# The last slot of a mixture-of-experts block: when the slot in front is added to its first chunk, and in which order the last two chunks are normalised

## Chip, cores and metric

The kernel runs on one core of a Trainium2 chip. The metric is the device time of one execution in microseconds (us), as the median of several executions. The engines are named as the profile names them: PE (TensorE, the matrix products), PEld (its weight loads), DVE (VectorE), ACT (ScalarE), POOL (GpSimd) and SP (SyncE, which here only issues transfers).

## What is computed

512 tokens of width 1024 pass through a mixer block, a layer norm, a mixture of 32 experts (two experts for each token) together with a gated per-layer term, and a last layer norm. Only the end of it matters here:

```python
h = _layernorm(DEEPNORM_ALPHA * h + mix, ln1_g[i], ln1_b[i])
moe = _hier_moe(h, ...)      # for each expert: act = silu(h @ gate) * (h @ up) * weight;  out += act @ down
ple = (p[i] @ w_ple[i]) * jax.nn.sigmoid(h @ w_pg[i] + b_pg[i])
h = _layernorm(DEEPNORM_ALPHA * h + moe + ple, ln2_g[i], ln2_b[i])
```

## The kernel before

The tokens stand in `tok` as four chunks of 128 rows by 1024 columns, float32. The experts are worked off in 12 slots of 128 gathered token rows; a slot holds the rows of a few experts side by side. For each slot `gate_up` multiplies the gathered rows with the gate and up weights in two halves (`kh` 0 and 1, each over four of the eight pieces of the width), `act` makes silu(gate) * up * weight, `atr` transposes it, and `down` multiplies it with the down weights into two banks of 512 columns each. After each bank ScalarE copies it out (`yh`, line 1105) and VectorE forms what the copy rounded away (`yl`, line 1107); the slot's result is the sum of the two.

`scatter(s, chunks)` adds the result of slot `s` back to the chunks: for each chunk and each half of 512 columns one product of a 0/1 matrix with `yh` (line 1142), one with `yl` (line 1144) and one VectorE addition to `tok` (line 1145). It is issued for the slot in front while the next slot is at work.

The last slot (`last_slot`, slot 11, with `p` = 10 the slot in front) is arranged by hand. The token rows that the last slot itself works on are put together separately, in the two banks `zr`, from their earlier share (`take`) and the slot's own products (`take_own`); for all other rows the four chunks of `tok` are complete as soon as slot `p` is added. The chunks are normalised and stored while the last slot's products go on. Each chunk needs: two statistics passes and an aggregation on VectorE (`ln_dve`), a square root on ScalarE (`ln_sqrt`), a reciprocal (`ln_rs`), and then the two passes that apply mean, scale, gain and offset, in one of two ways:

- `ln_pool`: `ln_nm` on VectorE (a 128x1 value), then for each 512 columns a pass on ScalarE (line 1392) and a multiplication on GpSimd (line 1393), and a GpSimd addition (line 1395). Chunk 0, chunk 1 and the first 512 columns of chunk 3 go this way. The second half of chunk 1 is called from inside `act`, behind the sigmoid.
- `affine_a` and `affine_b`: two VectorE passes, both with two inputs in the on-chip memory (lines 1400 and 1405). Chunk 2 and the last 512 columns of chunk 3 go this way.

At the end `put` writes chunk 3 by an indirect transfer issued from GpSimd; then the sums in `zr` are normalised on VectorE (lines 1465 to 1472) into `row`, and a second `put` writes these rows. The first `put` waits for both halves of chunk 3.

Each engine works through its instructions in the order in which the kernel's code issues them (`tc.manual_schedule()`), and waits for other engines by semaphores; so the order of the calls in `last_slot` is the order on every engine. The accumulation banks of the scatter products are three in turn, shared with those of `down`; a bank is free when VectorE has read it.

Of the kernel before, what the change touches and what calls it, by code (L numbers as in the profile page):

```python
# [140 lines left out]
def block_kernel(ctx: ExitStack, tc: tile.TileContext, I, out):  # L141
# [14 lines left out]
    def pst(tag, nm="", shape=(P, 512), dt=F32):  # L156
        _pi[0] += 1
        banks[tag].append(banks[tag].pop(0))
        return ps.tile(list(shape), dt, tag=f"b{banks[tag][-1]}", name=f"{tag}{_pi[0]}_{nm}")

    def sm(nm, *shape, dt=F32, tag=None, bufs=1):
        return small.tile([P, *shape], dt, tag=tag or nm, bufs=bufs, name=nm)
# [30 lines left out]
    def ln_part(key, src, h, n=2):  # L193
        if h == 0:
            stt_[key] = sm(f"st{key}", n, 6, tag=f"st{n}", bufs=4)
        V.bn_stats(stt_[key][:, h, :], src[:, h * (D // n):(h + 1) * (D // n)])
# [7 lines left out]
    def ln_rs(key):  # L204
        V.reciprocal(rst[key], rst[key])

    def ln_nm(key):
        nmt[key] = sm(f"nm{key}", 1, tag="nm", bufs=4)
        V.tensor_scalar(nmt[key], mvt[key][:, 0:1], rst[key], -1.0, OP.mult, OP.mult)
# [467 lines left out]
    def done(*keys):  # L677
        for k in keys:
            tag = W.pop(k)[1]
            if tag is None:  # L680
                continue
            if tag == "bc" and len(pieces) < 26:
                bc2.append(tmp("bc", 1, [P, 2, D], "bc2"))
            elif k[0] == "x" and k[2] == YK and not ytags:
                ytags.append(tag)
            else:
                free.append(tag)
        pump()
# [351 lines left out]
    def gate_up(s, lanes, kh, mid=None):  # L1040
        if kh == 0:
            gps[s] = pst("g" if s < NS else "u", f"gu{s}")
        g = gps[s]
        for k in range(4 * kh, 4 * kh + 4):
            if mid and k % 4 == 2:
                mid()
            for q, m, r in lanes:
                PE.matmul(g[q:q + m, :], xTs[s][:, k, q:q + m],  # L1048
                          W["x", r, kh][0][:, (k % 4) * 512:(k % 4 + 1) * 512],
                          start=(k == 0), stop=(k == KD - 1), tile_position=(0, q))  # L1050
        clk["pe"] += 3.7
        done(*[("x", r, kh) for r in dict.fromkeys(r for _, _, r in lanes)])

    def act(s, wsl, tkf, i, oh=None, sa=None):
        g = gps[s]
        sa = tmp("ct", 2, [P, 2, F], f"sa{s}") if sa is None else sa
        A.activation(sa[:, 0, :], g[:, 0:F], AF.Sigmoid)  # L1057
        if s == NS - 1:
            ln_pool(1, 512, D)
        V.tensor_mul(sa[:, 0, :], g[:, 0:F], sa[:, 0, :])  # L1060
        V.scalar_tensor_tensor(sa[:, 1, :], g[:, F:2 * F], wsl[:, i:i + 1], sa[:, 0, :], OP.mult, OP.mult)
        acts[s] = sa
        if s == NS - 1:
            return
        if s in DS:
            return
        ohs[s] = tmp("cv", 2, [P, T], f"oh{s}", F32R) if oh is None else oh
        V.tensor_scalar(ohs[s], C["iota"], tkf[:, i:i + 1], None, OP.is_equal)

    def atr(s, dst=None):  # L1070
        pt = pst("t", f"at{s}")
        for c in range(2):
            PE.transpose(pt[:, c * P:(c + 1) * P], acts[s][:, 1, c * P:(c + 1) * P], idn)  # L1073
        aTs[s] = tmp("full", 2, [P, 2, P], f"aT{s}") if dst is None else dst
        A.copy(aTs[s], pt[:, 0:2 * P].rearrange("p (c t) -> p c t", t=P))
# [58 lines left out]
    def scatter(s, cs=range(NC), mid=None, hs=(0, 1)):  # L1134
        yh, yl = ys[s]
        for c in cs:
            for h in hs:
                if mid and h:
                    mid()
                w = slice(h * 512, (h + 1) * 512)  # L1140
                o = pst("u", f"sc{s}{c}{h}")
                PE.matmul(o, ohs[s][:, c * P:(c + 1) * P], yh[:, w], start=True, stop=yl is None)  # L1142
                if yl is not None:
                    PE.matmul(o, ohs[s][:, c * P:(c + 1) * P], yl[:, w], start=False, stop=True)  # L1144
                V.tensor_add(tok[:, c, w], tok[:, c, w], o)  # L1145
            clk["pe"] += 1.15
# [213 lines left out]
    def take(key, rows, start=False):  # L1360
        for h in range(2):
            for i in range(2):
                PE.matmul(zr[h], sel[key], rows[i][:, h * 512:(h + 1) * 512], start=start and i == 0, stop=False)  # L1363

    def take_own(h):
        PE.matmul(zr[h], sel["own"], ys[NS - 1][:, h, :], start=False, stop=True)


    def ln_dve(c):

        key = f"2{c}"
        for h in range(2):
            ln_part(key, tok[:, c, :], h)
        mvt[key] = sm(f"mv{key}", 2, tag="mv", bufs=4)
        V.bn_aggr(mvt[key], stt_[key])
        nmt[key] = None

    def ln_sqrt(c):
        key = f"2{c}"
        rst[key] = sm(f"rs{key}", 1, tag="rs", bufs=4)  # L1380
        A.activation(rst[key], mvt[key][:, 1:2], AF.Sqrt, bias=eps_t)

    def ln_pool(c, lo, hi):

        key = f"2{c}"
        if nmt[key] is None:
            ln_nm(key)
        nm = nmt[key]
        for a in range(lo, hi, 512):
            b = min(a + 512, hi)  # L1390
            t = tok[:, c, a:b]
            A.activation(t, t, AF.Identity, bias=nm, scale=rst[key])
            G.tensor_mul(t, t, bc2[0][:, 0, a:b])
        t = tok[:, c, lo:hi]
        G.tensor_add(t, t, bc2[0][:, 1, lo:hi])

    def affine_a(c, lo=0, hi=D):

        t = tok[:, c, lo:hi]
        V.scalar_tensor_tensor(t, t, mvt[f"2{c}"][:, 0:1], bc2[0][:, 0, lo:hi], OP.subtract, OP.mult)  # L1400

    def affine_b(c, lo=0, hi=D):

        t = tok[:, c, lo:hi]
        V.scalar_tensor_tensor(t, t, rst[f"2{c}"], bc2[0][:, 1, lo:hi], OP.mult, OP.add)  # L1405
# [3 lines left out]
    def store(c, lo=0, hi=D):  # L1409
        stores.append(SP.dma_start(out[c * P:(c + 1) * P, lo:hi], tok[:, c, lo:hi]))  # L1410

    def put(to, rows):
        return G.indirect_dma_start(out=out, out_offset=bass.IndirectOffsetOnAxis(ap=to[:, 0:1], axis=0),
                                    in_=rows, in_offset=None, bounds_check=T - 1, oob_is_err=False)

    def last_slot(lanes):
        s = NS - 1
        p = s - 1
        A.activation(warm, eps_t, AF.Sqrt)

        def first():
            scatter(p, (0,))
            ln_dve(0)
            ln_sqrt(0)
            scatter(p, (1,))
            ln_rs("20")
            ln_pool(0, 0, D)
            store(0)

        gate_up(s, lanes, 0, first)  # L1430
        ln_dve(1)
        ln_sqrt(1)
        scatter(p, (2,))
        gate_up(s, lanes, 1)
        A.activation(warm, eps_t, AF.Sigmoid)
        ln_rs("21")
        ln_pool(1, 0, 512)
        ln_dve(2)
        act(s, wsl, tkf, s)
        scatter(p, (3,))  # L1440
        take(p, ys[p])
        atr(s)
        ln_sqrt(2)
        ln_dve(3)
        ln_sqrt(3)
        ln_rs("22")
        affine_a(2)
        affine_b(2)
        store(2)
        store(1)  # L1450
        ln_rs("23")
        ln_nm("23")
        affine_a(3, LNP)
        affine_b(3, LNP)
        down(s, lanes)
        ln_pool(3, 0, LNP)
        s3 = put(sel["to3"], tok[:, NC - 1, :])
        for d in stores:
            tc.declare_no_dep(s3.ins, d.ins, reason="rows of other chunks")
        for h in range(2):  # L1460
            take_own(h)
        key = "2r"
        stt_[key] = sm("st2r", 2, 6, tag="st2", bufs=4)
        for h in range(2):
            V.bn_stats(stt_[key][:, h, :], zr[h])
        ln_var(key)
        row = tmp("x0", 1, [P, D], "row")
        for h in range(2):
            t = row[:, h * 512:(h + 1) * 512]
            V.scalar_tensor_tensor(t, zr[h], mvt[key][:, 0:1], bc2[0][:, 0, h * 512:(h + 1) * 512], OP.subtract, OP.mult)  # L1470
        ln_rs(key)
        V.scalar_tensor_tensor(row, row, rst[key], bc2[0][:, 1, :], OP.mult, OP.add)
        tc.declare_no_dep(put(sel["to"], row).ins, s3.ins, reason="disjoint rows")
# [19 lines left out]
    for s in range(NS):  # L1493
        lanes = SLOTS[s]
# [88 lines left out]
LNP = 512  # L1583
# [30 lines left out]
```

## Time and profile before

| | us |
|---|---|
| median of 3 runs | 466.48 |
| lowest and highest run | 465.04, 468.22 |
| the profiled execution, its own time | 465.6 |
| its span, first to last instruction | 463.6 |
| PE busy | 428.5 (92% of the span) |
| DVE busy | 239.2 (52%) |
| POOL busy | 149.7 (32%) |
| ACT busy | 136.0 (29%) |
| mean granted TensorE clock | 0.982 of full speed |

The span starts with the first instruction and ends with the last; the time of the execution has 2.0 us more around it. Busy shares are averages over the whole program. Times of single instructions below are microseconds from the span's start.

### The profile page before, as it was taken

Reading aid. Unit: us, or ns where it says so; the run is one execution under the profiler, and the core shown is the slowest. Engines: PE = TensorE matmul, PEld = TensorE weight load, DVE = VectorE, ACT = ScalarE, POOL = GpSimd, SP = SyncE. Lnnn points to the kernel's source line nnn. Section 1 sums busy time; section 2 is a strip of 40 time slices with the busy share of each in tenths; the row PEclk is TensorE's granted clock in tenths of the full one; section 3 lists DMA queues with packets and bytes.
Section 4 is the critical chain, followed back from the end, with each engine's and each line's share of the span. In section 5 each row is a group of like instructions: output and inputs, shape, how many; then the busy total and the mean of one; then the engine's idle time right before and its main releaser. Section 6 shows DMA issues by size and latency. Waiting matters only on the chain.

```text
span 463.6 us, 6886 instructions
## 1 busy us (share of the span) xinstructions
PE 428.5 (92%) x2583; PEld 287.6 (62%) x2583; DVE 239.2 (52%) x463; ACT 136.0 (29%) x240; POOL 149.7 (32%) x129
## 2 busy tenths in 40 slices
PE   7899977999999998899999997999999999899980
PEld 6798865788899997653556362745465544445330
DVE  4938599879764578513315010110122469735695
ACT  4453502432410377411111120111420142231360
POOL 2556499334600760130001010110040133242094
PEclk9999998999999999999999998999999999999995
DMA  8822203422769669669999999999999999999213
GB/s 270 351 92 91 92 0 98 176 90 92 260 264 386 222 258 345 246 240 418 423 419 419 420 417 426 419 419 420 422 414 418 418 420 413 417 419 396 99 57 142
DMA packets 25117, 136.85 MB, mean 295 GB/s; under 512 B 4167, under 2 KB 4427, under 8 KB 11768
## 3 DMA queue, kind: packets, MB, share of 16 engines
q1 hardware_dynamic: 20456, 124.64, 67.0%
q0 software_dynamic: 3760, 8.05, 4.6%
q10 hardware_dynamic: 864, 3.67, 2.0%
q8 instruction: 22, 0.36, 0.3%
q14 instruction: 15, 0.12, 0.1%
HBM read 134.61 MB, written 6.82 MB: 305 GB/s over the span
## 4 chain that ended last, share of the span: by engine, by line
PE 24%; DMA 23%; issue 5%; DVE 1%; POOL 1%; SPq 1%; ACT 1%; POOLq 0%; DVEq 0%; ACTq 0%
DMA w_x<-wx_in 20%; PE g_gu L1048 10%; PE q_pg L818 4%; PE u_y L1094 3%; DMA yg<-yd,yix 3%; PE u_sc L1142 2%; PE t_xt L1037 1%; PE u_sc L1144 1%; PE q_zr L1363 1%; PE q_pg L810 1%; SPq L670 0%; SPq L664 0%; DVE tok L1405 0%; PE t_at L1073 0%; POOL yg L1126 0%
## 5 line engine op out<-in xcount | busy, mean ns | idle before, releaser
L1048 PE MATMUL g_gu<-w_x,xT 128*32 128x512 f32 (+1 forms) x544 | 88.1, 610 | 5.5 <-DMA w_x<-wx_in 5.2
L363 PE MATMUL u_u<-hTh,ws 128*128 128x512 f32 (+1 forms) x320 | 67.1, 353 | 2.4 <-ACT hTh L344 1.4
L1048 PEld LDWEIGHTS g_gu<-w_x,xT 128*32 128x32 f32 (+1 forms) x544 | 25.5, 119 | 58.1 <-issue 44.9
L363 PEld LDWEIGHTS u_u<-hTh,ws 128*128 128x128 f32 x320 | 53.8, 193 | 11.0 <-ACT hTh L344 1.6
L818 PE MATMUL q_pg<-w_pg,h1T 128*128 128x256 f32 x240 | 57.3, 381 | 0.0
L1145 DVE TENSOR_TENSOR tok<-tok,u_sc 128x512 f32<-128x512 f32 x56 | 35.1, 680 | 29.1 <-PE u_sc L1144 28.9
L818 PEld LDWEIGHTS q_pg<-w_pg,h1T 128*128 128x128 f32 x240 | 44.5, 190 | 8.1 <-issue 2.5
L1028 POOL DMA_INDIRECT xrow<-h1d,idxm x12 | 12.2, 1020 | 87.7 <-PE t_xt L1037 76.0
L1094 PE MATMUL u_y<-w_x,aT 128*32 128x512 f32 (+1 forms) x272 | 40.3, 596 | 0.0
L829 POOL TENSOR_TENSOR tok<-tok,sgp 128x256 f32<-128x256 f32 x16 | 11.5, 723 | 81.5 <-DVE sgp L828 74.1
L187 PE MATMUL u_o<-ws,yTh 128*128 128x256 f32 x128 | 36.7, 287 | 0.6 <-ACT yTh L446 0.6
L189 PE MATMUL u_o<-ws,yTl 128*128 128x256 f32 x128 | 36.3, 284 | 0.6 <-DVE yTl L447 0.6
L188 PE MATMUL u_o<-ws,yTh 128*128 128x256 f32 x128 | 36.2, 283 | 0.0
L363 PE MATMUL u_u<-hTl,ws 128*128 128x512 f32 (+1 forms) x160 | 35.0, 349 | 0.9 <-DVE hTl L348 0.9
L1060 DVE TENSOR_TENSOR sa<-g_gu,sa 128x256 f32<-128x256 f32 x12 | 5.1, 423 | 53.2 <-ACT sa L1057 53.2
L1057 ACT ACTIVATE sa<-g_gu 128x256 f32<-128x256 f32 x12 | 4.6, 382 | 93.5 <-PE g_gu L1048 93.5
L248 DVE TENSOR_TENSOR ws<-raw,ws 128x1024 fp32r<-128x1024 f32 (+1 forms) x19 | 25.7, 1385 | 10.1 <-ACT ws L245 10.1
L363 PEld LDWEIGHTS u_u<-hTl,ws 128*128 128x128 f32 x160 | 27.1, 189 | 5.4 <-DVE hTl L348 1.5
L828 DVE TENSOR_TENSOR sgp<-q_pg,sgp 128x256 f32<-128x256 f32 x15 | 6.3, 423 | 42.0 <-ACT sgp L825 41.9
L245 ACT CAST ws<-raw 128x1024 fp32r<-128x1024 f32 x23 | 23.1, 1046 | 8.6 <-DMA raw<-wout_in 5.4
L1142 PE MATMUL u_sc<-y,oh 128*128 128x512 f32 x56 | 25.5, 456 | 0.0
L1094 PEld LDWEIGHTS u_y<-w_x,aT 128*32 128x32 f32 (+1 forms) x272 | 11.7, 117 | 22.1 <-issue 21.0
(280 smaller groups left out, 699.6 us busy)
## 6 DMA issues: line engine op xcount, KB each, us to landing
w_x<-wx_in SPq DMA_DIRECT2D x89, 1024.0 KB, 17.3
raw<-win_in SPq DMA_DIRECT2D x6, 1024.0 KB, 4.7
w_half<-wx_in SPq DMA_DIRECT2D x12, 512.0 KB, 14.3
raw<-wout_in SPq DMA_DIRECT2D x4, 1024.0 KB, 5.2
w_pg<-wpg_in SPq DMA_DIRECT2D x4, 1024.0 KB
raw<-win_in SPq DMA_DIRECT2D x4, 512.0 KB
bc<-rows_in SPq DMA_DIRECT2D x4, 512.0 KB
yd<-yrows ACTq DMA_DIRECT2D x4, 512.0 KB
```

Of the source, the lines that this page charges most:

```text
L187: PE.matmul(o, lh, rh, start=start, stop=False)
L188: PE.matmul(o, lh, rl, start=False, stop=False)
L189: PE.matmul(o, ll, rh, start=False, stop=stop)
L245: copy(wsp[n][0][j], raws[n][:, j, :])
L248: eng.tensor_sub(wsp[n][1][j][:, ks], raws[n][:, j, ks], wsp[n][0][j][:, ks].bitcast(F32))
L363: PE.matmul(o[:, ns], (l if p == 2 else h)[j][:, kn], (hTl if p == 1 else hTh)[k][:, ns], start=i == 1, stop=i == 3 * KD)
L818: PE.matmul(g, h1T[:, k, cs], W["pg", j, 0][0][:, k * 256:(k + 1) * 256], start=(k == 0), stop=False)
L1028: G.indirect_dma_start(out=xgs[s], out_offset=None, in_=h1d, in_offset=bass.IndirectOffsetOnAxis(ap=idx[:, i:i + 1], axis=0), bounds_check ...
L1048: PE.matmul(g[q:q + m, :], xTs[s][:, k, q:q + m], W["x", r, kh][0][:, (k % 4) * 512:(k % 4 + 1) * 512], start=(k == 0), stop=(k == KD - 1) ...
L1094: PE.matmul(yp[h][q:q + m, :], aTs[s][:, c, q:q + m], W["x", r, 2][0][:, c * D + h * 512:c * D + (h + 1) * 512], start=(c == 0), stop=(c = ...
L1142: PE.matmul(o, ohs[s][:, c * P:(c + 1) * P], yh[:, w], start=True, stop=yl is None)
L1145: V.tensor_add(tok[:, c, w], tok[:, c, w], o)
```

## The change

Three things are put in another order; no instruction is added or taken away.

1. `scatter(p, (0,))`, the statistics and the square root of chunk 0 come ahead of the first half of the last slot's gate products. Before, they came after two of the four pieces of that half. The addition to chunk 1, and what followed it, stays in the middle of that half.
2. The reciprocal and the `ln_nm` of chunk 1 are called ahead of the second half of the gate products rather than behind it.
3. The reciprocal and the `ln_nm` of chunk 3, and its `ln_pool`, come ahead of the two VectorE passes of chunk 2. Before, the first two came behind those passes, and the `ln_pool` came behind `down`.

```diff
-        def first():
-            scatter(p, (0,))
-            ln_dve(0)
-            ln_sqrt(0)
+        def second_chunk():
             scatter(p, (1,))
             ln_rs("20")
             ln_pool(0, 0, D)
             store(0)
 
-        gate_up(s, lanes, 0, first)
+        scatter(p, (0,))
+        ln_dve(0)
+        ln_sqrt(0)
+        gate_up(s, lanes, 0, second_chunk)
         ln_dve(1)
         ln_sqrt(1)
         scatter(p, (2,))
+        ln_rs("21")
+        ln_nm("21")
         gate_up(s, lanes, 1)
         A.activation(warm, eps_t, AF.Sigmoid)
-        ln_rs("21")
         ln_pool(1, 0, 512)
         ln_dve(2)
         act(s, wsl, tkf, s)
...
         ln_rs("22")
+        ln_rs("23")
+        ln_nm("23")
+        ln_pool(3, 0, LNP)
         affine_a(2)
         affine_b(2)
         store(2)
         store(1)
-        ln_rs("23")
-        ln_nm("23")
         affine_a(3, LNP)
         affine_b(3, LNP)
         down(s, lanes)
-        ln_pool(3, 0, LNP)
         s3 = put(sel["to3"], tok[:, NC - 1, :])
```

## Rows read from the trace of the kernel before

**Rows 1.** Busy time of each engine by stretch: length, busy time (instructions), clock, DMA.

```profile
398.00:400.00 2.00, 1.30 (x5) 0.81 (x6) 2.00 (x5) 0.00 (x0) 0.00 (x0) 1.00 1.03 413
439.00:443.00 4.00, 4.00 (x19) 1.30 (x18) 3.93 (x9) 3.90 (x7) 2.89 (x3) 1.00 0.00 0
```

**Rows 2.** Instructions in time, VectorE, last slot: start, duration, line, [idle before <- releaser].

```profile
433.03 0.69 DVE L1107 TENSOR_TENSOR y<-u_y,y 128x512 fp32r<-128x512 f32 x1 [1.03 <-ACT y L1105]
434.78 1.28 DVE L1145 TENSOR_TENSOR tok<-tok,u_sc 128x512 f32<-128x512 f32 x2 [1.06 <-PE u_sc L1144]
...
437.42 1.23 DVE L1145 TENSOR_TENSOR tok<-tok,u_sc 128x512 f32<-128x512 f32 x2
...
443.30 0.42 DVE L1060 TENSOR_TENSOR sa<-g_gu,sa 128x256 f32<-128x256 f32 x1
...
447.15 0.17 DVE L205 RECIPROCAL rs<-rs 128x1 f32<-128x1 f32 x1 [0.28 <-ACT rs L1381]
447.24 1.45 DVE L1400 SCALAR_TENSOR_TENSOR tok<-tok,mv,bc 128x1024 f32<-128x1024 f32 x1
448.80 2.11 DVE L1405 SCALAR_TENSOR_TENSOR tok<-tok,rs,bc 128x1024 f32<-128x1024 f32 x1
...
451.14 1.44 DVE L1400 SCALAR_TENSOR_TENSOR tok<-tok,mv,bc 128x512 f32<-128x512 f32 x1
452.61 1.63 DVE L1405 SCALAR_TENSOR_TENSOR tok<-tok,rs,bc 128x512 f32<-128x512 f32 x1
454.17 1.28 DVE L1465 BATCH_NORM_STATS2 st2r<-q_zr 128x6 f32<-128x512 f32 x2
```

**Rows 3.** Instructions in time, TensorE, last slot.

```profile
432.19 1.89 PE L1048 MATMUL g_gu<-w_half,xT 128*64 128x512 f32 x8
...
434.01 0.50 PE L1142 MATMUL u_sc<-y,oh 128*128 128x512 f32 x1
...
436.19 1.94 PE L1048 MATMUL g_gu<-w_half,xT 128*64 128x512 f32 x8
...
438.05 0.50 PE L1142 MATMUL u_sc<-y,oh 128*128 128x512 f32 x1
...
439.18 3.65 PE L1048 MATMUL g_gu<-w_half,xT 128*64 128x512 f32 x16
```

**Rows 4.** Instructions in time, ScalarE, last slot.

```profile
442.90 0.37 ACT L1057 ACTIVATE sa<-g_gu 128x256 f32<-128x256 f32 x1
```

**Rows 5.** The chain that ended last, in order of time: start, duration, what.

```profile
444.89 0.23 PE t_at L1073 x2
...
445.53 1.28 ACT L1381
```

**Rows 6.** Instructions in time, an earlier slot, where a scatter product waits for VectorE.

```profile
397.96 1.28 DVE L1107 TENSOR_TENSOR y<-u_y,y 128x512 fp32r<-128x512 f32 x2
398.70 0.50 PE L1144 MATMUL u_sc<-y,oh 128*128 128x512 f32 x1 [1.43 <-DVE y L1107]
...
399.30 0.50 PE L1144 MATMUL u_sc<-y,oh 128*128 128x512 f32 x1
...
399.64 0.40 PE L1142 MATMUL u_sc<-y,oh 128*128 128x512 f32 x1
```

**Rows 7.** Instructions in time, GpSimd, last slot.

```profile
440.04 2.52 POOL L1393 TENSOR_TENSOR tok<-tok,bc 128x512 f32<-128x512 f32 x2 [17.66 <-ACT tok L1392]
...
446.34 1.27 POOL L1395 TENSOR_TENSOR tok<-tok,bc 128x512 f32<-128x512 f32 x1
447.57 2.25 POOL L1393 TENSOR_TENSOR tok<-tok,bc 128x512 f32<-128x512 f32 x1
449.90 2.12 POOL L1395 TENSOR_TENSOR tok<-tok,bc 128x512 f32<-128x512 f32 x1
452.21 1.49 POOL L1393 TENSOR_TENSOR tok<-tok,bc 128x512 f32<-128x512 f32 x1 [0.19 <-ACT tok L1392]
453.77 1.59 POOL L1395 TENSOR_TENSOR tok<-tok,bc 128x512 f32<-128x512 f32 x1
```

## Prediction

> **What bounds the kernel now.** The change touches only the last 30 us, so I read that stretch and nothing of the shares of the whole. First the busy time by stretch: while the last slot's products run, VectorE is busy for 3.93 of 4.00 us and TensorE for all 4.00 [rows 1]. Two engines look like the bound at once, and the question is which of them the other waits for. So I next read VectorE's own instructions with their idle times [rows 2]: from 434.78, where the slot in front begins to be added to chunk 0, until the end there is one idle time worth naming, 0.28 us at 447.15, for ScalarE. Ahead of 434.78 there are 1.06 us without work, and that is what the first edit reaches for.
>
> But VectorE works in order, and in the middle of its list stands a multiplication that needs the finished gate products. It starts at 443.30 [rows 2]; the sigmoid that releases it starts at 442.90 [rows 4], and the products in front of that started at 439.18 and take 3.65 us, to 442.83 [rows 3]. So at 442.9 there is no slack on either side: TensorE's order sets that point as strictly as VectorE's. Behind it the chain of waits runs over TensorE again: chunk 3's scatter, four `take` products, the transposes at 444.89, ScalarE's copy, a table load at 445.53 that ends at 446.81 [rows 5], the square roots, and VectorE's reciprocal at 447.15 [rows 2]. From 447.24 to 454.24 VectorE makes its four passes over chunks 2 and 3 and shares something with GpSimd (below); then it normalises the last rows, which takes the same time in both kernels, as does the write behind them. **The end therefore moves with the end of the fourth VectorE pass, 454.24**, and that moves with the gate products and with GpSimd.
>
> **Edit 1, chunk 0 ahead of the gate products: TensorE.** Before, the first eight gate products followed `down` at 432.19 and covered the time in which VectorE made `yl` of the second half of the slot in front, 433.03 to 433.72 [rows 2, 3]. After, chunk 0's products stand there. The first half can go at once; the product with the second `yl` cannot start before 433.72. An earlier slot shows the hand-over: two such VectorE instructions end at 399.24, the product starts at 399.30 and the next one at 399.64 [rows 6]. So here: product at 433.78, the first gate product at 434.12. From then the pieces have the lengths of before [rows 3]: eight gate products take 1.86 us (436.19 to 438.05), a chunk's four scatter products 1.13 us (438.05 to 439.18). After: gate from 434.12, chunk 1 from 435.98, gate from 437.11, chunk 2 from 438.97, second half from 440.10 instead of 439.18. **TensorE comes 0.92 us later** out of the same work. Bounds: the hand-over may cost nothing (0.06 less), and the hand-over pattern of four scatter products may carry a further change-over of 0.1 each way; 0.8 to 1.1.
>
> **Edit 1, VectorE.** It starts earlier: chunk 0's additions at 433.75, 1.03 us ahead. The second one has its product 0.4 us behind 433.78, in time. The next additions began 2.64 us behind the first ones before (434.78 to 437.42), so VectorE is ready for chunk 1 at 436.39; but chunk 1's products start only at 435.98, and an addition follows them by 0.77 us (434.01 to 434.78), so it starts at 436.75: 0.67 ahead of before [rows 2, 3]. Chunk 2 costs a further 0.1 in the same way (438.97 plus 0.77 is 439.74). VectorE then has its statistics done some 0.6 us sooner, at about 442.7, and **waits for the gate products until 443.30 plus 0.92, 444.22**. Everything it won is given back in an idle time of 1.5 us, and 0.92 more. Behind the multiplication the whole chain over transposes, copy, table load and square roots is in the same order as before, so the reciprocal comes at 447.15 plus 0.92, 448.07.
>
> **Edit 2, chunk 1's two small instructions.** Between the old and the new place stand only products and a ScalarE instruction; on VectorE they follow chunk 2's additions and precede chunk 2's statistics either way, and no queue sees a new order. Nothing, as long as calls set the order of each engine alone.
>
> **Edit 3, chunk 3's scale and its GpSimd part ahead of chunk 2's passes.** To cost it, the four passes must be understood. A VectorE pass of 1024 columns ends 1.09 us after the GpSimd instruction beside it ended (447.57 plus 2.25 is 449.82; 448.80 plus 2.11 is 450.91); the next GpSimd one ends 1.11 us after that (452.02), the next pass, of 512 columns, 0.56 after that (452.58), then GpSimd 1.12 (453.70), VectorE 0.54 (454.24), GpSimd 1.12 (455.36) [rows 2, 7]. They take strict turns. An undisturbed GpSimd instruction lasts 1.27 [rows 7]. So a pass costs its 0.55 or 1.09 us plus one GpSimd turn of 1.12 if GpSimd has work, and the sum for VectorE is four passes plus the number of GpSimd turns in between. Before, that number was three.
>
> After: VectorE issues the reciprocal at 448.07, the moved pair (0.23 to 0.3 us, from the gap between 450.91 and 451.14 [rows 2]), and the first pass at about 448.4. GpSimd started 0.67 sooner and ran without a break from 440.04 to 447.57 before [rows 7], so its chunk-1 multiplication runs from 446.90 to 448.17, and its last chunk-1 addition is issued at 448.23, 0.17 ahead of the pass. If it is first: 449.50; pass 450.59; chunk 3's multiplication 451.71; pass 452.80; chunk 3's addition 453.92; passes 454.48 and 455.1. If the VectorE pass is first: 449.49, 450.61, 451.70, 452.82, 453.38, 454.50, 455.06. Three turns both times, so who wins this close race hardly matters: **the last pass ends 0.8 to 0.9 us later than 454.24**. The moved pair is hidden when GpSimd is first. Before, it was hidden as well, behind the turn that ended at 452.02.
>
> Bounds of this term: if GpSimd were a whole instruction further on, chunk 1 would be finished and only two turns would be left. That saves 1.1 us, and the end comes 0.2 us sooner than before. If hand-overs are longer (one more tenth at each of four), 1.3 later.
>
> What else moves: ScalarE makes chunk 3's pass ahead of its copies of the last slot's result, which may hold the first copy for 0.3 us; VectorE reads those sums only behind its fourth pass, nearly 3 us later. The store of chunk 2, and chunk 1's behind it on SP, go out 1.9 us later, behind which only `put`'s transfers come. The first `put` loses its wait for GpSimd's last addition (455.36 before) and waits for the pass at 455.1 instead; it stays ahead of the last rows. None of it is on the path.
>
> **Sum.** Nothing is saved at the end, 0.9 us are added: 465.6 plus 0.9 is 466.5 for the profiled execution, which lies 0.9 below the median of the runs. For the median, 466.48 plus 0.9: **467.4 us**. That is 0.2%, less than the 1% or so that a measurement of this kernel can tell from no change.
>
> **Rivals.**
> - *VectorE is the bound and keeps its lead.* Then the end comes 0.7 to 1.0 us sooner, 465.6 in the median. It speaks for it that VectorE has hardly a gap in 20 us. It needs the gate products by 442.7, while TensorE had them at 442.83 without the wait for `yl` in front; it decides from the point where TensorE's order costs less than nothing. 0.10.
> - *GpSimd is done with chunk 1 before the first pass*, two turns instead of three: 466.3. Its lead would have to be 1.1 us larger than the 0.67 worked out. 0.17.
> - *The pause drops TensorE's clock.* After, TensorE waits for at most a microsecond ahead of 433.78. At the lower of its two levels (1.2 instead of 2.4 GHz) the 11 us of products from 434.12 to the transposes would take 11 us more: 478. In the earlier slot TensorE was idle for 1.43 us before 398.70 and the stretch from 398 to 400 shows the granted clock at 1.00, 2.4 GHz [rows 1, 6]; so I take nothing. [...] 0.02.
> - *The edit does not do what it says*: chunk 0 is not added sooner, because its second half hangs on `yl`. That is half true and inside the forecast: the addition starts 1.03 us sooner, the products behind it 0.92 later.
> - Something at the end collides (the later stores with the two `put`s): 469 and more, 0.03.
>
> **How the numbers follow.** The forecast (0.5 to 1.3 later) has 0.68, the rivals the chances named. The terms alone span 0.2 us sooner to 1.3 later, 466.3 to 467.8; single runs lie up to 1.7 us from their median, a new median perhaps 1.2, so the range is 465.1 to 469.0; the first rival's 465.6 lies inside too. Only a clock drop or a collision leaves the 1%: slower by more than that 0.03, faster 0.01, the same 0.96.
>
> **What the profile after would show.** TensorE idle for some 0.7 us ahead of the second `yl` product near 433.8; the second half of the gate products near 440.1; VectorE's first addition near 433.75, and an idle time above 1 us ahead of its multiplication at line 1060, now near 444.2; the first pass of line 1400 lasting about 2.2 us if GpSimd is first, 1.1 to 1.4 if not; the statistics of line 1465 near 455.0. If line 1060 starts at 443.3 or sooner, the TensorE step is wrong; if the four passes meet two GpSimd turns, the last step is.

## Result, and the profile after

The changed kernel takes **470.0 us** in the median of 20 runs, the kernel before 467.5 in the median of as many; the ratio is 1.0055 with a 95% interval from 1.0031 to 1.0078, so 1.4 to 3.6 us more. The forecast was 467.4 and a loss of 0.9 us: the direction holds, the size does not, and 470.0 lies above the range of 465.1 to 469.0. Run a second time beside the kernel before, the ratio was 1.0032 (1.0006 to 1.0058), so 0.3 to 2.7 us more.

(One of the earlier kernel's 20 runs took 1079 us and is left out of the ratio, as disturbed runs are.)

The profiled execution has a span of 466.8 us instead of 463.6. To see how much of these 3.2 us belongs to the edits, every trace below is read from one mark: the start of the first `yl` subtraction of the slot in front (line 1107), the last VectorE work that no edit touches. It is at 431.31 before and at 433.33 after. So 2.02 us had been lost before any moved instruction ran; from the mark to the end it is 32.29 us before and 33.47 after. **The last slot lost 1.18 us.**

The other 2.02 us lie far ahead of it. Busy time by stretch, first the kernel before, then the changed one (length, busy time and number of instructions of PE, PEld, DVE, ACT, POOL, granted clock, DMA share, GB/s):

```profile
180.00:190.00 10.00, 8.87 (x59) 7.17 (x59) 7.49 (x38) 5.98 (x10) 1.33 (x3) 1.00 0.70 273
190.00:200.00 10.00, 8.22 (x78) 4.76 (x78) 3.45 (x18) 3.29 (x6) 2.28 (x4) 1.00 0.51 188
```

```profile
180.00:190.00 10.00, 9.30 (x52) 7.37 (x51) 5.97 (x27) 5.79 (x9) 0.31 (x2) 0.83 0.65 258
190.00:200.00 10.00, 8.46 (x68) 5.30 (x69) 4.57 (x25) 3.58 (x7) 2.17 (x2) 0.83 0.54 187
```

TensorE was granted its full clock, 2.4 GHz, in this stretch of the one execution and 0.83 of it on average, so 1.2 GHz for a part of the time, in the other. Ahead of it TensorE did the same in both: products of 32 columns and fewer, with idle times of 0.60 and 0.65 us for VectorE. Two groups of the same products that follow, first in the kernel before, then in the changed one:

```profile
183.48 3.62 PE L818 MATMUL q_pg<-w_pg,h1T 128*128 128x256 f32 x16
...
196.10 3.64 PE L1048 MATMUL g_gu<-w_x,xT 128*32 128x512 f32 x32 [0.24 <-ACT xT L1038]
```

```profile
183.14 5.20 PE L818 MATMUL q_pg<-w_pg,h1T 128*128 128x256 f32 x16
...
197.42 4.90 PE L1048 MATMUL g_gu<-w_x,xT 128*32 128x512 f32 x32
```

The changed execution is 0.34 us ahead at the first group; the two groups together take it 2.84 us longer. What the granted clock does differs from run to run of the same program: among the 20 runs of the changed kernel the five with a mean granted clock of 0.979 or more took 467.2 to 468.4 us, the six with 0.968 or less 469.8 to 472.6. And the place of the mark differs as much where nothing differs in the program: the two traces of edit 3 alone (below) have it at 434.98 and at 431.95. No edit touches this part.

VectorE in the last slot of the changed kernel, in order of time, against [rows 2]:

```profile
433.33 0.69 DVE L1107 TENSOR_TENSOR y<-u_y,y 128x512 fp32r<-128x512 f32 x1 [2.23 <-ACT y L1105]
435.05 0.69 DVE L1107 TENSOR_TENSOR y<-u_y,y 128x512 fp32r<-128x512 f32 x1 [1.03 <-ACT y L1105]
435.66 1.36 DVE L1145 TENSOR_TENSOR tok<-tok,u_sc 128x512 f32<-128x512 f32 x2
...
438.88 1.28 DVE L1145 TENSOR_TENSOR tok<-tok,u_sc 128x512 f32<-128x512 f32 x2 [0.41 <-PE u_sc L1144]
...
446.35 0.42 DVE L1060 TENSOR_TENSOR sa<-g_gu,sa 128x256 f32<-128x256 f32 x1 [1.43 <-ACT sa L1057]
...
450.21 0.35 DVE L205 RECIPROCAL rs<-rs 128x1 f32<-128x1 f32 x2 [0.28 <-ACT rs L1381]
...
450.73 2.07 DVE L1400 SCALAR_TENSOR_TENSOR tok<-tok,mv,bc 128x1024 f32<-128x1024 f32 x1
452.90 2.10 DVE L1405 SCALAR_TENSOR_TENSOR tok<-tok,rs,bc 128x1024 f32<-128x1024 f32 x1
454.93 1.75 DVE L1400 SCALAR_TENSOR_TENSOR tok<-tok,mv,bc 128x512 f32<-128x512 f32 x1
456.71 0.75 DVE L1405 SCALAR_TENSOR_TENSOR tok<-tok,rs,bc 128x512 f32<-128x512 f32 x1
457.38 1.29 DVE L1466 BATCH_NORM_STATS2 st2r<-q_zr 128x6 f32<-128x512 f32 x2
```

Chunk 0 is added 2.33 us behind the mark instead of 3.47, and then VectorE idles: 0.41 us for chunk 1's products, 1.43 us for the gate products. TensorE shows why, against [rows 3]:

```profile
435.07 0.49 PE L1142 MATMUL u_sc<-y,oh 128*128 128x512 f32 x1
435.79 0.51 PE L1144 MATMUL u_sc<-y,oh 128*128 128x512 f32 x1 [0.23 <-DVE y L1107]
436.23 1.94 PE L1048 MATMUL g_gu<-w_half,xT 128*64 128x512 f32 x8
...
442.23 3.65 PE L1048 MATMUL g_gu<-w_half,xT 128*64 128x512 f32 x16
```

The product with the second `yl` waits for the subtraction, which ends at 435.74, and the second half of the gate products starts 8.90 us behind the mark instead of 7.87: 1.03 later. GpSimd, against [rows 7]:

```profile
449.08 1.28 POOL L1393 TENSOR_TENSOR tok<-tok,bc 128x512 f32<-128x512 f32 x1
450.44 1.27 POOL L1395 TENSOR_TENSOR tok<-tok,bc 128x512 f32<-128x512 f32 x1
451.80 2.12 POOL L1393 TENSOR_TENSOR tok<-tok,bc 128x512 f32<-128x512 f32 x1
454.00 2.12 POOL L1395 TENSOR_TENSOR tok<-tok,bc 128x512 f32<-128x512 f32 x1
```

Its last chunk-1 addition, 450.44 to 451.71, is ahead of VectorE's first pass (issued at 450.73, ended at 452.80), and the strict turns of the prediction go on from there: VectorE to 452.80, GpSimd 453.92, VectorE 455.00, GpSimd 456.12, VectorE 456.68. Three turns. The fourth pass meets none and ends at 457.46. The statistics of the last rows start 24.05 us behind the mark instead of 22.86. What follows them takes 9.4 us in both kernels.

### The profile page after: what moved, and what is told of

Read it like the earlier page. It is cut to its first block, busy times and chain, and to the rows that moved or that the text cites. A ratio compares the mean times of both kernels' runs of the same rounds, so it can differ in the third digit from the quotient of the medians.

```text
span 466.8 us, 6886 instructions
## 1 busy us (share of the span) xinstructions
PE 434.1 (93%) x2583; PEld 289.5 (62%) x2583; DVE 238.9 (51%) x463; ACT 136.3 (29%) x240; POOL 149.4 (32%) x129
## 4 chain that ended last, share of the span: by engine, by line
PE 34%; DMA 14%; issue 5%; DVE 2%; POOL 1%; ACT 1%; SPq 0%; POOLq 0%; DVEq 0%; ACTq 0%
PE g_gu L1048 14%; DMA w_x<-wx_in 11%; PE q_pg L818 5%; PE u_y L1094 5%; DMA yg<-yd,yix 3%; PE t_xt L1037 2%; PE u_sc L1142 2%; PE u_sc L1144 2%; PE q_pg L810 2%; PE q_zr L1363 1%; DVE tok L1400 1%; DVE tok L1405 1%; PE t_at L1073 0%; POOL yg L1126 0%; DVE y L1107 0%
## 5 line engine op out<-in xcount | busy, mean ns | idle before, releaser
L818 PE MATMUL q_pg<-w_pg,h1T 128*128 128x256 f32 x240 | 58.9, 389 | 0.0
L818 PEld LDWEIGHTS q_pg<-w_pg,h1T 128*128 128x128 f32 x240 | 45.6, 195 | 8.7 <-issue 2.5
L189 PEld LDWEIGHTS u_o<-ws,yTl 128*128 128x128 f32 x128 | 24.5, 192 | 0.8 <-DVE yTl L447 0.8
```

The source lines that it names most:

```text
L189: PE.matmul(o, ll, rh, start=False, stop=stop)
L818: PE.matmul(g, h1T[:, k, cs], W["pg", j, 0][0][:, k * 256:(k + 1) * 256], start=(k == 0), stop=False)
```

## Experiments

All times in the text below are counted from the mark of the trace they belong to, unless a fence or a row ahead of the prediction shows them. "Last stretch" is the time from the mark to the end. A turn is a GpSimd instruction that a VectorE pass waits for. What they gave, from one profile each, and the ratio to the kernel before on the same chip:

| kernel | second gate half starts | first VectorE pass issued | GpSimd turns it meets | statistics of the last rows | mark to end | ratio (95%) |
|---|---|---|---|---|---|---|
| before | 7.87 | 15.93 | 3 | 22.86 | 32.29 | |
| changed | 8.90 | 17.40 | 3 | 24.05 | 33.47 | 1.0055 (1.0031 to 1.0078) |
| changed, again | 8.88 | 17.39 | 3 | 24.04 | 33.53 | 1.0032 (1.0006 to 1.0058) |
| edit 2 alone | 7.86 | 15.91 | 3 | 22.86 | 32.29 | 0.9998 (0.9970 to 1.0025) |
| edit 1 alone | 8.88 | 16.95 | 1 | 22.12 | 31.63 | 0.9993 (0.9963 to 1.0023) |
| edit 3 alone | 7.86 | 16.36 | 4 | 24.09 | 33.52 | 1.0015 (0.9988 to 1.0042) |
| edit 3 alone, again | 7.86 | 16.37 | 4 | 24.09 | 33.55 | one run |
| edit 3, pair alone | 7.87 | 16.35 | 4 | 24.09 | 33.57 | 1.0039 (1.0016 to 1.0061) |
| pair between the passes | 7.87 | 15.93 | 3 | 22.87 | 32.30 | 0.9988 (0.9962 to 1.0015) |
| changed, chunk 3 on VectorE | 8.88 | 17.39 | 1 | 23.25 | 32.75 | 1.0007 (0.9977 to 1.0037) |
| changed, without `yl` | 8.14 | 16.63 | 3 | 23.41 | 32.91 | 1.0001 (0.9968 to 1.0034) |
| one piece, with edit 3 | 8.08 | 16.57 | 3 | 23.32 | 32.83 | 1.0004 (0.9979 to 1.0029) |
| one piece | 8.11 | 16.16 | 1 and a third | 21.67 | 31.18 | 0.9975 (0.9945 to 1.0004) |
| one piece, again | 8.11 | 16.18 | 1 and a third | 21.66 | 31.16 | 0.9958 (0.9935 to 0.9982) |

Where the same order of instructions was profiled twice, the last column but one agrees within 0.06 us. So the mark tells tenths apart, where the ratios, with single runs several us apart, hardly tell 1 us.

### The edits one by one

Edit 2 alone:

```diff
         scatter(p, (2,))
+        ln_rs("21")
+        ln_nm("21")
         gate_up(s, lanes, 1)
         A.activation(warm, eps_t, AF.Sigmoid)
-        ln_rs("21")
```

> Only edit 2, the reciprocal and the ln_nm of chunk 1 ahead of the second half of the gate products. Every engine's list of instructions keeps its order, so this is the kernel before under another name. Theory A (the loss sits in the last slot, and what the medians show beyond it comes from the granted clock of the first 200 us, which differs from run to run): the stretch from the first yl subtraction of the slot in front (line 1107) to the end of the span takes 32.3 us as before, within 0.2; the time differs from the kernel before by less than 0.3%, and runs with a granted clock near 0.98 are the faster ones. Theory B (the edits shift something ahead of the last slot): the same here, as nothing is moved.

It is the kernel before: 32.29, ratio 0.9998.

Edit 1 alone:

```diff
-        gate_up(s, lanes, 0, first)
+        scatter(p, (0,))
+        ln_dve(0)
+        ln_sqrt(0)
+        gate_up(s, lanes, 0, second_chunk)
```

> Only edit 1, chunk 0 ahead of the gate products. Theory A: TensorE waits for the second yl, the second half of the gate products starts 1.0 us later counted from the first yl subtraction, the GpSimd turns stay three, and the last stretch takes 33.2 to 33.5 us instead of 32.3; the whole is 0.2 to 0.3% slower than before. Rival A2 (most of the loss is edit 3's): the last stretch is within 0.4 of 32.3. Theory B: 0.5% slower with a last stretch of only 33.3.

Here theory A fell; of the rival the reason holds, not its number. TensorE is as late as in the changed kernel (8.88), but the last stretch is not 33.3 us: it is 31.63, **0.66 shorter than before**. VectorE's passes, then GpSimd's instructions:

```profile
450.92 1.27 DVE L1400 SCALAR_TENSOR_TENSOR tok<-tok,mv,bc 128x1024 f32<-128x1024 f32 x1
452.29 2.11 DVE L1405 SCALAR_TENSOR_TENSOR tok<-tok,rs,bc 128x1024 f32<-128x1024 f32 x1
...
454.64 0.74 DVE L1400 SCALAR_TENSOR_TENSOR tok<-tok,mv,bc 128x512 f32<-128x512 f32 x1
455.42 0.75 DVE L1405 SCALAR_TENSOR_TENSOR tok<-tok,rs,bc 128x512 f32<-128x512 f32 x1
```

```profile
449.70 1.27 POOL L1393 TENSOR_TENSOR tok<-tok,bc 128x512 f32<-128x512 f32 x1
451.06 2.27 POOL L1395 TENSOR_TENSOR tok<-tok,bc 128x512 f32<-128x512 f32 x1
455.71 1.58 POOL L1393 TENSOR_TENSOR tok<-tok,bc 128x512 f32<-128x512 f32 x1 [2.39 <-ACT tok L1392]
```

The first pass finds the way free. The second gives GpSimd one turn. Then chunk 1 is finished, chunk 3's GpSimd part is not ready before 455.7 because its scale is made behind chunk 2's passes, and VectorE's two passes over chunk 3 take 0.74 and 0.75 instead of 1.44 and 1.63 [rows 2]. Two turns are saved: VectorE comes later and GpSimd sooner, so that chunk 1's multiplication is over ahead of the first pass; and chunk 3's, with its late scale, finds no pass left to hold up.

Edit 3 alone, profiled twice:

```diff
         ln_rs("22")
+        ln_rs("23")
+        ln_nm("23")
+        ln_pool(3, 0, LNP)
         affine_a(2)
         affine_b(2)
         store(2)
         store(1)
-        ln_rs("23")
-        ln_nm("23")
...
         down(s, lanes)
-        ln_pool(3, 0, LNP)
```

> Only edit 3, chunk 3's scale and its GpSimd part ahead of chunk 2's passes. Theory A (strict turns of VectorE and GpSimd): VectorE issues the moved pair at the old time of its first pass, GpSimd's list keeps its order, three GpSimd turns lie between the four passes; the last stretch is 32.2 to 32.7 us, the whole within 0.1% of before. Rival A2 (most of the loss is edit 3's): 33.0 us or more. Theory B: within 0.1% as well.

> Edit 3 alone once more, for a second look at the race of a tenth of a us between VectorE's first pass and GpSimd's chunk-1 multiplication. Theory P: if GpSimd is first again, the last stretch is 33.5 us again; if VectorE is first, one turn falls behind the last pass and it is 32.3 to 32.6. Anything else speaks against strict turns.

Not 32.2 to 32.7 but 33.52, and 33.55 the second time: **edit 3 alone costs 1.23 us**. VectorE and GpSimd:

```profile
451.34 2.25 DVE L1400 SCALAR_TENSOR_TENSOR tok<-tok,mv,bc 128x1024 f32<-128x1024 f32 x1
453.70 2.10 DVE L1405 SCALAR_TENSOR_TENSOR tok<-tok,rs,bc 128x1024 f32<-128x1024 f32 x1
455.73 1.75 DVE L1400 SCALAR_TENSOR_TENSOR tok<-tok,mv,bc 128x512 f32<-128x512 f32 x1
457.51 1.63 DVE L1405 SCALAR_TENSOR_TENSOR tok<-tok,rs,bc 128x512 f32<-128x512 f32 x1
```

```profile
451.25 1.27 POOL L1393 TENSOR_TENSOR tok<-tok,bc 128x512 f32<-128x512 f32 x1
452.60 2.13 POOL L1395 TENSOR_TENSOR tok<-tok,bc 128x512 f32<-128x512 f32 x1
454.69 2.24 POOL L1393 TENSOR_TENSOR tok<-tok,bc 128x512 f32<-128x512 f32 x1
457.00 1.59 POOL L1395 TENSOR_TENSOR tok<-tok,bc 128x512 f32<-128x512 f32 x1
```

Before, VectorE's first pass was issued at 447.24 and GpSimd's chunk-1 multiplication at 447.57 [rows 2, 7]: VectorE was first by a third of a us and the multiplication waited (2.25 us). Here the moved pair holds the pass back to 451.34, the multiplication is issued at 451.25, and by nine hundredths it is GpSimd that is first. Every one of the four passes now waits for a turn.

The changed kernel again:

> The changed kernel once more. Theory A: last stretch 33.3 to 33.6 us, so 1.0 to 1.3 us more than the kernel before in the same stretch; the time beside the kernel before is 0.2 to 0.4% longer, and the rest of the earlier 0.55% goes with the granted clock. Theory B: 0.5 to 0.6% longer again, in runs with the same granted clock as before.

33.53 against 32.29, as in the first profile; the ratio came out at 1.0032.

### Which part of edit 3

The pair of small instructions moved, `ln_pool` left in its old place:

```diff
         ln_rs("22")
+        ln_rs("23")
+        ln_nm("23")
         affine_a(2)
         affine_b(2)
         store(2)
         store(1)
-        ln_rs("23")
-        ln_nm("23")
```

> Only half of edit 3: chunk 3's reciprocal and ln_nm ahead of chunk 2's passes, its ln_pool left behind down. Theory P (the pair costs because it lets GpSimd have the turn first): VectorE issues the first pass 0.43 us later than before, 16.36 instead of 15.93 from the first yl subtraction, GpSimd's chunk-1 multiplication is issued at 16.27, a tenth ahead of it, and chunk 3's GpSimd part is ready in time for every turn; four GpSimd turns lie between the passes, the last stretch takes 33.4 to 33.6 us as with all of edit 3. Rival Q (the early ln_pool costs, by its place in ScalarE's and GpSimd's lists): 32.3 to 32.8 us here.

33.57 us and four turns: the early place of `ln_pool` adds nothing. Then the pair was put between the two passes of chunk 2, where it holds up no first pass but makes the scale almost as early:

```diff
         affine_a(2)
+        ln_rs("23")
+        ln_nm("23")
         affine_b(2)
         store(2)
         store(1)
-        ln_rs("23")
-        ln_nm("23")
```

> The kernel before with chunk 3's reciprocal and ln_nm between the two passes of chunk 2, so that the first pass isn't held up but chunk 3's scale still comes early. Theory P (what counts is that the first pass is issued ahead of GpSimd's chunk-1 multiplication): first pass at 15.93 as before, three turns, statistics of the last rows at 22.8 to 22.95, last stretch 32.2 to 32.4 us. Rival (the early scale releases chunk 3's GpSimd part into VectorE's passes): a fourth turn and 33.4 us or more.

32.30 us, first pass at 15.93 and first, three turns. What edit 3 costs on top of the kernel before is thus the 0.42 us by which two 128x1 instructions delay the first pass into a lost race.

### What the turns and the wait cost in the changed kernel

Chunk 3 wholly on VectorE:

```diff
-        ln_pool(3, 0, LNP)
...
-LNP = 512
+LNP = 0
```

> The changed kernel with chunk 3 normalised wholly on VectorE, so that GpSimd has nothing of chunk 3: two passes of 1024 columns instead of 512, and no GpSimd turns for chunk 3. If turns are strict (theory P): the first pass still waits for the last chunk-1 addition, then four passes of 1.09 us run back to back; two turns of 1.12 us go, 1.1 us of VectorE work come, and the statistics of the last rows start 1.0 to 1.3 us sooner than in the changed kernel, at 22.8 to 23.1 from the first yl subtraction; last stretch 32.2 to 32.5 us. Rival R (two engines share a rate, each slowed in proportion): the doubled VectorE work costs its 1.1 us and the passes get back less, statistics at 23.5 or later.

```profile
449.84 2.04 DVE L1400 SCALAR_TENSOR_TENSOR tok<-tok,mv,bc 128x1024 f32<-128x1024 f32 x1
451.99 1.28 DVE L1405 SCALAR_TENSOR_TENSOR tok<-tok,rs,bc 128x1024 f32<-128x1024 f32 x1
453.19 1.28 DVE L1400 SCALAR_TENSOR_TENSOR tok<-tok,mv,bc 128x1024 f32<-128x1024 f32 x1
454.50 1.28 DVE L1405 SCALAR_TENSOR_TENSOR tok<-tok,rs,bc 128x1024 f32<-128x1024 f32 x1
```

The first pass waits as before, the others run at 1.28 us each although two of them are twice as wide as they were. Statistics at 23.25, 0.80 sooner than in the changed kernel: a little short of the 1.0 expected, since passes back to back follow one another by 1.2 to 1.3 us and not by 1.09, but on the side of the turns; a rate shared in proportion would have given 23.5 or later. VectorE does more work and is done sooner.

The product of the second `yl` for chunk 0 left out (half of chunk 0 then gets only the rounded result of the slot in front):

```diff
-                PE.matmul(o, ..., yh[:, w], start=True, stop=yl is None)
-                if yl is not None:
+                last = yl is None or (s == NS - 2 and c == 0 and h == 1)
+                PE.matmul(o, ..., yh[:, w], start=True, stop=last)
+                if not last:
```

> The changed kernel without the product of the second yl for chunk 0 (its low part is left out there: the half of chunk 0 gets the rounded result of the slot in front only), so that TensorE waits only for ScalarE's copy. If the wait for yl is what makes TensorE late: the first gate product comes at 2.1 to 2.2 from the first yl subtraction instead of 2.9, VectorE's multiplication at 12.2 to 12.4 instead of 13.0, its reciprocal at 16.1 to 16.2 instead of 16.9; three GpSimd turns as in the changed kernel, so the statistics of the last rows at 23.2 to 23.4 instead of 24.05 and a last stretch of 32.6 to 32.9 instead of 33.5: the wait is worth 0.7, and what remains above the kernel before is edit 3. Rival (TensorE's later start is absorbed by the turns): 33.3 or more.

The first gate product comes at 2.16 instead of 2.90, the reciprocal at 16.12 instead of 16.88, the statistics at 23.41 instead of 24.05: the wait with its product is worth 0.74 us on TensorE and 0.64 at the end, at the edge of what was expected. It reaches the end nearly whole, with edit 3 in place and the turns at three.

### Chunk 0 between the pieces

The wait disappears without leaving anything out if one of the four gate pieces stands in front of chunk 0:

```diff
-            if mid and k % 4 == 2:
-                mid()
+            if mid and k % 4 in mid:
+                mid[k % 4]()
...
-        def first():
+        def first_chunk():
             scatter(p, (0,))
             ln_dve(0)
             ln_sqrt(0)
+
+        def second_chunk():
             scatter(p, (1,))
...
-        gate_up(s, lanes, 0, first)
+        gate_up(s, lanes, 0, {1: first_chunk, 2: second_chunk})
```

> Edit 1 in another form and without edits 2 and 3: chunk 0's scatter comes behind one of the four gate pieces (four products) instead of two or none, chunk 1's behind two as before. If TensorE's wait for the second yl is what delays the gate products: no wait is left, the second half of the gate products starts at most 0.4 us later than before (7.9 to 8.3 from the first yl subtraction, against 8.9 in the changed kernel), VectorE starts on chunk 0 at 2.4 to 2.7 instead of 3.5. With GpSimd half a us sooner, the first pass meets one turn and the second one; chunk 3's GpSimd part is held back until VectorE is through. Statistics of the last rows at 21.2 to 21.8, last stretch 30.7 to 31.4 us, so 0.9 to 1.6 less than the kernel before and 0.2 to 0.9 less than edit 1 alone; whole 0.2 to 0.35% faster. If the wait for yl was not the delay, the second half starts near 8.9 here too and nothing is won over edit 1 alone.

> Chunk 0 behind one gate piece, without edits 2 and 3, once more: last stretch 31.2 us against 32.3 before, 0.2 to 0.3% faster than the kernel before; the earlier ratio was 0.9975.

From the second of the two, TensorE, then VectorE, then GpSimd:

```profile
435.72 1.03 PE L1048 MATMUL g_gu<-w_half,xT 128*64 128x512 f32 x4
436.68 0.50 PE L1142 MATMUL u_sc<-y,oh 128*128 128x512 f32 x1
437.02 0.40 PE L1144 MATMUL u_sc<-y,oh 128*128 128x512 f32 x1
...
437.82 1.08 PE L1048 MATMUL g_gu<-w_half,xT 128*64 128x512 f32 x4
```

```profile
451.02 1.59 DVE L1400 SCALAR_TENSOR_TENSOR tok<-tok,mv,bc 128x1024 f32<-128x1024 f32 x1
452.71 2.11 DVE L1405 SCALAR_TENSOR_TENSOR tok<-tok,rs,bc 128x1024 f32<-128x1024 f32 x1
...
455.06 0.74 DVE L1400 SCALAR_TENSOR_TENSOR tok<-tok,mv,bc 128x512 f32<-128x512 f32 x1
455.83 0.75 DVE L1405 SCALAR_TENSOR_TENSOR tok<-tok,rs,bc 128x512 f32<-128x512 f32 x1
```

```profile
450.25 1.27 POOL L1393 TENSOR_TENSOR tok<-tok,bc 128x512 f32<-128x512 f32 x1
451.60 2.13 POOL L1395 TENSOR_TENSOR tok<-tok,bc 128x512 f32<-128x512 f32 x1
456.13 1.58 POOL L1393 TENSOR_TENSOR tok<-tok,bc 128x512 f32<-128x512 f32 x1 [2.39 <-ACT tok L1392]
```

TensorE has no wait in front of the second `yl`, and its second gate half starts 0.24 us later than before instead of 1.03. The first pass waits a third of a turn (a whole one was expected), the second a whole one, chunk 3's none. The last stretch is 31.16 to 31.18 us, 1.1 less than before; measured, 0.9975 and 0.9958 of the kernel before, the second clear of 1 (0.9935 to 0.9982). This is the version to keep: about 1 us better than the kernel before and more than 2 in the last stretch than the changed one.

With edit 3 added:

> Chunk 0 behind one gate piece, together with edit 3. Theory P: the moved pair puts the first pass at 16.6 from the first yl subtraction, three turns follow (chunk 1's last addition, chunk 3's two) instead of one and a half without edit 3; statistics of the last rows at 23.2 to 23.4, last stretch 32.6 to 32.9, so 1.5 more than the same kernel without edit 3 (31.2). Rival Q (edit 3 costs only where TensorE is late): 31.2 to 31.7.

```profile
451.14 1.28 DVE L1400 SCALAR_TENSOR_TENSOR tok<-tok,mv,bc 128x1024 f32<-128x1024 f32 x1
```

```profile
451.32 2.23 POOL L1395 TENSOR_TENSOR tok<-tok,bc 128x512 f32<-128x512 f32 x1
453.50 2.25 POOL L1393 TENSOR_TENSOR tok<-tok,bc 128x512 f32<-128x512 f32 x1
```

32.83 us, three turns, 1.65 more than without it. Here no race is lost: VectorE is first and its first pass is free. What costs is the early scale. Chunk 3's multiplication follows chunk 1's last addition without a break, where without edit 3 GpSimd waits 2.39 us for it, and both of chunk 3's GpSimd instructions meet a pass. In the changed kernel, too, the two turns more than with edit 1 alone are chunk 3's. So edit 3 costs 1.2 us on top of the kernel before, 1.9 on top of edit 1 (31.63 to 33.5) and 1.65 here: with TensorE late or not.

## Why the prediction was off

- **Where the miss of 2.6 us lies.** About 1.0 is the base of the sum: 466.48 is the median of three runs, and the twenty runs of the kernel before give 467.5. On that base the same working gives 468.4 and a range of 466.1 to 470.0. About 0.3 is the last slot (1.18 measured, 0.9 forecast). The other 1.3 stand outside the last slot and are taken up under the size of the whole.
- **Edit 1, TensorE: right.** Forecast 0.92 us later, measured 1.03; the wait for the second `yl` is the cause (0.74 us go with its product, 0.79 with one piece in front).
- **Edit 1, VectorE: right.** The lead is spent in an idle time of 1.43 us ahead of the multiplication at line 1060 (1.5 forecast).
- **Edit 2: right.** Nothing.
- **The strict turns: right,** and the basis of all that follows. The Trainium skill (SBUF — State Buffer, section "Who interferes with whom") says that a VectorE instruction with two inputs in SBUF contends with a GpSimd instruction that reads SBUF, that the port pair they share is an exclusive lock, and that the order of issue decides who is blocked. The traces agree: free, VectorE's first pass takes 1.27 us (edit 1 alone); issued 0.33 us ahead of GpSimd's multiplication it takes 1.45 [rows 2, 7]; issued 0.09 us behind, it takes 2.25 (edit 3 alone).
- **Edit 3: the step that failed.** It was priced at nothing: "the moved pair is hidden". Alone it costs 1.23 us, on top of edit 1 from 1.84 to 1.90. "Three turns both times" holds for the two edits together, and with edit 3 in place it holds whoever wins the race: GpSimd is first in the changed kernel, VectorE with one piece and edit 3, and both meet three. So the sum in the last slot came out near. But the loss was put down to TensorE's lateness. Turns were counted for the sum of the edits and never for each alone: alone, edit 1 meets one turn and wins 0.66 us in spite of TensorE, and edit 3 meets four. The rival "GpSimd is done with chunk 1 before the first pass" looked at the right quantity, the number of turns, but took GpSimd's lead for the only thing that changes it. The time at which chunk 3's scale is ready changes it as well.
- **The last slot's 0.3 us.** GpSimd's lead is 0.51 us instead of 0.67, so that its last chunk-1 addition ends 0.19 us later than forecast (18.38 behind the mark instead of 18.19); and the last pass ends 0.78 us behind the third (456.68 to 457.46) where 0.62 was forecast. The pair (0.43 us rather than 0.3) and TensorE's tenth do not enter: the first pass, issued at 17.40, waits for that addition.
- **The size of the whole.** The median moved by 2.5 us, twice what the last slot shows; the prediction gave "a new median perhaps 1.2" of its own spread. In the profiled pair the other 2.02 us stand ahead of the mark, with the lower clock between 180 and 200 us. The repeat gave 0.3 to 2.7 us, which takes in 1.2; the first comparison, 1.4 to 3.6, does not quite. On the chip of the repeat the changed kernel's median was 468.4 and that of the kernel before 468.0. As no instruction ahead of the mark changes its place, I take the difference for the clock's chance over a set of runs; that it is chance alone was not shown.
- The first rival (VectorE keeps its lead) and the drop of the clock by the pause are refuted: line 1060 starts 1.03 us later, and after the pause sixteen gate products take 3.65 us as before, with a granted clock of 1.00 from 430 to 450 us.

## What to carry to other kernels

Where two engines exclude each other instruction by instruction, count the turns that each long instruction meets, for each edit alone and for all together; a few tenths of a us on the issue of the first can decide a whole instruction's length, and the effects of two edits need not add (here 0.66 won and 1.23 lost made 1.18 lost). A result that is fetched early can let a second engine into the way of the first: chunk 3's late scale kept GpSimd out of VectorE's way. And ahead of work that waits for a neighbour, put just as much independent work as covers the wait: one piece was enough, none cost 0.8 us, two gave away VectorE's time.

## What the runs showed of the hardware

Nine hundredths of a us in the order of issue came out the same way in every profile of that order (three of three), and the last 32 us repeat within 0.06 us, while whole runs of one program differ by 5 us with the granted clock: in the 20 runs of the changed kernel from 467.2 us at 0.980 to 472.6 at 0.965. The same sixteen products of line 818 take 3.62 us where the clock was 1.00 and 5.20 where it was 0.83 on average.
